# One layer of a gated DeltaNet: the planner's periods become five chains, weights' low halves move to VectorE, an exponential is cut in four, and one more PSUM bank is counted

## The chip, the cores and the metric

The kernel runs on one core of a Trainium2 chip. The metric is the device time of one execution in microseconds; the runs of before took 1149.68, 1152.65 and 1159.56 us, so their median is 1152.65.

## The reference, cut to what matters

With a depth of one only the gated DeltaNet layer runs, on one sequence of 1024 tokens of width 1024, and a final RMS norm follows.

```python
h = rms_norm(x) * (1 + scale(c)) + shift(c)
qkv, z, b, a = split(h @ w_in)                       # q, k: 8 heads; v, z: 16 heads; all of 128
q, k, v = split(silu(causal_depthwise_conv(qkv)))    # 4 taps
q, k = l2norm(q) * 128 ** -0.5, l2norm(k)            # each for two heads of v
beta, g = sigmoid(b), -exp(a_log) * softplus(a + dt_bias)
# by chunk: decay = exp(gc_i - gc_j) below the diagonal, gc the running sum of g
T = inverse(I + strictly_lower((k * beta) @ k.T * decay))
u, w = T @ (v * beta), T @ (k * beta * exp(gc))
# scan over the chunks, state S of 128 x 128 for each head
v_new = u - w @ S
o = (q * exp(gc)) @ S + lower(q @ k.T * decay) @ v_new
S = S * exp(g_last) + (k * exp(g_last - gc)).T @ v_new
o = rms_norm(o) * norm_w * silu(z)
out = rms_norm(x + gate(c) * (o @ w_out))
```

## The kernel before, in words

Chunks are 128 tokens here instead of 64, which changes no result, so the scan of a head has 8 steps. Heads of v go in pairs that share one head of q and k; a pair is a group, and there are 8 groups, G = 0 to 7. Matrices in float32 that need precision are split in a high and a low half in a faster format, and each projection is three products (high by high, high by low, low by high).

Ahead of the groups stand the norm, the modulation and the first projections. Then, for each group:

- `project` (from L591) makes one block of 128 columns for half of the tokens: 24 products of 128x512 into a bank pj (L598). A group has 6 such columns: k and q (`proj_kq`), two of v (`values`), two of z (`out_gate`). `loader` brings the weights: a DMA, ScalarE's high half whi (L586), GpSimd's low half wlo (L587), two of each for a column.
- `Conv` (L537 to L561): ScalarE copies the bank and scales it by one tap, VectorE adds three taps (L557), ScalarE does the SiLU (L561). Values are then transposed on TensorE (L813).
- `norms`: VectorE adds the gates to the mask em (L641), ScalarE takes the exponential of em, 128x2048 at once (L644), and k and q are transposed (L659, L667) for their squares.
- `stage_a`: products of k with k and q (L704), the matrix to be inverted, and the inverse of its 32x32 blocks by 62 short VectorE instructions on tm, tb and ua, each waiting for the one before (L733, L736). This is what the prediction calls the inversion chain. `levels` puts the blocks together on TensorE (L766 to L797), for each half of the tokens.
- `scan`: in each step k @ S into ks (L940), r on VectorE (L943), T @ r into ts (L963), vd (L967) and vh, q @ S into the bank oq (L973), the new state (L982, L987). The second product of a step, into the other half of oq (L910), comes in the next step, and VectorE sums both in o (L913). Then o is normalised over ScalarE, VectorE and GpSimd (L918 to L923), transposed on TensorE into pot (L892) and multiplied with z.

What sets the order: nothing is left to the hardware or the compiler. A planner (`Order`, from L62) runs while the program is built. It keeps a clock `now` for TensorE and a queue for each other engine, with a cost and a rank for each instruction, and emits the instruction of an engine whose planned start comes first, the lowest rank among equals. The work is written as generators, each of which yields a condition (`done`: planned as finished; `free`: a bank counted as free); `drive` steps the first generator whose condition holds. Each engine executes its instructions in the order that came out, whatever the real times are.

Before the change `drive` is called once for each period: the scan of group G, `stage_a` and `values` of G+1 and `proj_kq` of G+2 are given together, and the next period's generators start when all of them are over; only columns of z run on. When the projections are over, the products with the first four blocks of w_out (`early`, L1067) fill TensorE beside the last scan. The rest of w_out follows, 576 products.

Of the kernel before, what the change touches and what calls it, by code (L numbers as in the profile page):

```python
# [17 lines left out]
P = 128  # L18
# [12 lines left out]
RG = 1  # L31
LEV1 = (0, 7)
# [7 lines left out]
LATS, LAT, LATP, DMA = 50, 200, 320, 2800  # L40
# [21 lines left out]
class Order:  # L62
# [67 lines left out]
def gdn_layer(ctx: ExitStack, tc: tile.TileContext, x, c, ada_w, ada_b, norm_g, w_in, conv_w, a_log, dt_bias,  # L130
# [438 lines left out]
    def loader():  # L569
        while True:  # L570
# [9 lines left out]
            for k4 in range(0, KT, 4):  # L580
# [6 lines left out]
                ops.append(pool(lambda raw=raw, ks=ks, hi=hi, lo=lo: nc.gpsimd.tensor_tensor(  # L587
                    lo[:, ks], raw, hi[:, ks].bitcast(F32), op=ALU.subtract), 1290, a, holds=r))
# [22 lines left out]
    class Group:  # L611
        def __init__(self, gi):
# [4 lines left out]
            self.nop, self.TTop = [], {}  # L617

    def proj_kq(gi, G, old):
        G.kq = []  # L620
        for j, ct in ((0, 8 + gi), (1, gi)):
# [8 lines left out]
    def norms(gi, G):  # L630
# [3 lines left out]
        yield lambda: hasattr(order, "gate") and done(*order.gate, order.gc)  # L634
# [9 lines left out]
        G.emop = act(lambda: nc.scalar.activation(em, em, AF.Exp), 1820, *e, table="exp")  # L644
# [42 lines left out]
    def stage_a(gi, G, old):  # L687

        kq, ats = G.kq, []
        if not hasattr(G, "normed"):  # L690
            yield from norms(gi, G)
# [3 lines left out]
        for hf in range(NHALF):  # L695
            em, brk = G.em[hf], G.brk[hf]

            at, ops = None, []
            for j in range(4):
                js = slice(j * P, (j + 1) * P)  # L700
                yield lambda: done(G.emop, G.nop[hf][3]) and free("tr") and (not old or not old.ats or old.inverted[hf])
# [43 lines left out]
    def levels(gi, G, hf, old):  # L745
# [6 lines left out]
        yield lambda: not order.lock and (not (hf and old) or done(old.passed[0]))  # L752
        order.lock = True
# [45 lines left out]
        order.lock = False  # L799
# [4 lines left out]
    order.lock = False  # L804

    def values(gi, G, more):
# [13 lines left out]
        def tiles():  # L820
            for h in range(2):
                ct = 16 + 2 * gi + h
                cv = Conv(ct)
                for hf in range(NHALF):
                    if h == 0:
                        G.vtok.append(cp.tile([P, 4, 2, P], F32, name="vtok", tag="vtok", bufs=3))
                    ps, ph = yield from project(ct * P, hf, hf == NHALF - 1)
                    vT = cp.tile([P, TH], F32, name="vT", tag="vT", bufs=VB)
# [29 lines left out]
    def out_gate(head, G):  # L858

        for hf in range(NHALF):  # L860
            ps, ph = yield from project(Z0 + head * P, hf, hf == NHALF - 1)
            sz = cp.tile([P, TH], F32, name="sz", tag="sz")

            def store(hf=hf, sz=sz):
# [4 lines left out]
                            holds=ph))  # L869
            yield None  # L870

    def scan(gi, G):

        h0 = 2 * gi
        st = cp.tile([P, 2, P], F32, name="st", tag="st", bufs=1)
        late = []

        zs = {}

        def fetch():  # L880

            for n, *_ in late:
                if n not in zs and len(zs) < ZB and G.gated[n // 4] == 2:
                    z = cp.tile([P, 2, P], F32, name="z", tag="z", bufs=ZB)
                    zs[n] = z, load(lambda n=n, z=z: nc.sync.dma_start(
                        out=z, in_=z_dram[h0:h0 + 2, :, n * P:(n + 1) * P].rearrange("h e t -> e h t")))

        def finish():
            n, o, op = late.pop(0)
            pot, held = bank("pot", (P, 2, P)), order.hold("pot", 1)  # L890
            for h in range(2):
                nc.tensor.transpose(pot[:, h], o[:, h], ident)  # L892
            order.now += M2
            oT, stored = cp.tile([P, 2, P], F32, name="oT", tag="oT", bufs=OB), order.hold("oT", 1)
            z, zo = zs.pop(n)
            a = act(lambda: nc.scalar.mul(oT, pot, normw_c), 470, holds=held)  # L896
            b = pool(lambda: nc.gpsimd.tensor_tensor(oT, oT, z, op=ALU.mult), 800, a, zo)  # L897
            load(lambda: nc.sync.dma_start(
                out=o_dram[h0:h0 + 2, :, n * P:(n + 1) * P].rearrange("h e t -> e h t"), in_=oT), b, holds=stored)
            fetch()  # L900

        def can_finish():
            fetch()
            return late and late[0][0] in zs and done(late[0][2]) and free("pot") and order.avail("oT", OB)

        def second(n, po, vh, vo, o, oo):
# [5 lines left out]
            if n > 0:  # L912
                d = vec(lambda: nc.vector.tensor_tensor(o, o, po[:, 1], op=ALU.add), 256, *oo)  # L913
            else:
                d = vec(lambda: nc.vector.tensor_copy(o, po[:, 1]), 256)
# [8 lines left out]
            late.append((n, o, d))  # L924
            fetch()

        pend = sto = None
        for n in range(NT):
# [3 lines left out]
            while len(late) > LAG:  # L932
                yield can_finish
                finish()
# [4 lines left out]
            if n > 0:  # L939
# [7 lines left out]
                if len(late) > 2 and can_finish():  # L947
                    finish()
# [43 lines left out]
        while late:  # L992
            yield can_finish
            finish()
# [236 lines left out]
    with tc.manual_schedule(engines=ORDERED(nc)):  # L1231
# [9 lines left out]
        for gi in range(-1, HQ):  # L1241
# [8 lines left out]
            if gi + 1 < HQ:  # L1250
                if gi < 0:
                    streams.append(streams0)
# [91 lines left out]
```

## Time and profile before

| what | value |
|---|---|
| runs | 1149.68, 1152.65, 1159.56 us |
| profiled execution | 1154.56 us, its span 1152.8 us |
| granted TensorE clock, mean | 0.97 |
| TensorE, VectorE, ScalarE, GpSimd busy | 1075.8, 757.8, 542.7, 440.1 us |
| as shares of the span | 93%, 66%, 47%, 38% |
| chain that ended last, by engine | TensorE 43%, VectorE 23%, ScalarE 11%, DMA 8%, GpSimd 6% |

Engines work side by side, so the shares do not add up. A matmul's end is modelled, and so a wait of TensorE is partly covered in the table by the matmul before it; from start to start it shows whole. Idle time of another engine counts only where TensorE waits for it.

### The profile page before, as it was taken

To read this page: it belongs to the slowest core of one execution; us is meant where nothing else is said; L and a number is where in the kernel's file an instruction comes from. 1 tells how busy PE (TensorE), PEld (TensorE's weight loads), DVE (VectorE), ACT (ScalarE), POOL (GpSimd) and SP (SyncE) were. 2 spreads that over 40 slices of the span, in tenths; PEclk is the share of its full clock that TensorE was granted. 3 is DMA by queue.
4 is the path that set the end of the run, shared out by engine and by line. 5 is a ranking of instruction groups with operands and counts; after the bars stand their busy time and mean duration, and the time that the engine had idled before them with its cause. 6 is when DMAs were issued, how large, how long until landed. Compare 5 with 4: busy or idle time off the path is not lost.

```text
span 1152.8 us, 18300 instructions
## 1 busy us (share of the span) xinstructions
PE 1075.8 (93%) x6295; PEld 859.8 (75%) x6295; DVE 757.8 (66%) x1913; ACT 542.7 (47%) x1415; POOL 440.1 (38%) x530
## 2 busy tenths in 40 slices
PE   7999998989999999899989998999999889999997
PEld 7877786867787777677867786778787657788785
DVE  5458963697789757776686678577767766413514
ACT  6457921443662346336623743374356424424523
POOL 3351321352352115313622452154215234844643
PEclk9899997999999889999999999999999979999999
DMA  9812142233154322421423052215212474335441
GB/s 286 224 37 91 42 119 69 69 102 95 40 150 120 84 78 67 122 69 47 119 61 110 27 148 56 75 39 144 65 56 70 115 231 134 101 114 182 153 128 73
DMA packets 187555, 118.43 MB, mean 103 GB/s; under 512 B 59669, under 2 KB 166470, under 8 KB 186438
## 3 DMA queue, kind: packets, MB, share of 16 engines
q1 hardware_dynamic: 186960, 117.15, 35.7%
q8 instruction: 50, 0.82, 0.3%
q14 instruction: 43, 0.35, 0.1%
q10 hardware_dynamic: 502, 0.10, 0.0%
HBM read 91.98 MB, written 25.24 MB: 102 GB/s over the span
## 4 chain that ended last, share of the span: by engine, by line
PE 43%; DVE 23%; ACT 11%; DMA 8%; issue 6%; POOL 6%; SPq 2%; DVEq 0%; ACTq 0%; POOLq 0%
PE pj L598 20%; DVE tm L733 5%; DVE tb L736 5%; PE pj L1067 4%; DVE vT L557 3%; DMA ua<-D 2%; DVE em L641 2%; DMA woraw<-in_gdn_w_out 2%; POOL wolo L206 2%; PE tr L704 2%; PE tr L797 2%; PE tr L789 2%; ACT tr L662 1%; ACT tr L669 1%; DVE kq L557 1%
## 5 line engine op out<-in xcount | busy, mean ns | idle before, releaser
L587 POOL TENSOR_TENSOR wlo<-wraw,whi 128x512 fp32r<-128x512 f32 x88 | 120.1, 1380 | 301.0 <-ACT whi L586 291.3
L733 DVE TENSOR_TENSOR tm<-tb,ua 128x126 f32<-128x126 f32 (+22 forms) x248 | 81.2, 327 | 25.3 <-DMA ua<-D 18.9
L557 DVE SCALAR_TENSOR_TENSOR kq<-xb,taps,kq 128x512 f32<-128x512 f32 x96 | 76.4, 804 | 22.3 <-ACT kq L554 19.2
L736 DVE TENSOR_TENSOR tb<-tb,tm 128x126 f32<-128x126 f32 (+22 forms) x248 | 82.2, 331 | 6.9
L557 DVE SCALAR_TENSOR_TENSOR vT<-xb,taps,vT 128x512 f32<-128x512 f32 x96 | 82.1, 855 | 5.0 <-ACT vT L554 3.9
L598 PE MATMUL pj<-h0hia,whi 128*128 128x512 f32 x184 | 77.6, 422 | 1.3 <-ACT kq L554 1.3
L598 PE MATMUL pj<-h0loa,whi 128*128 128x512 f32 x184 | 78.6, 427 | 0.0
L598 PE MATMUL pj<-h1lob,whi 128*128 128x512 f32 x184 | 77.4, 421 | 0.0
L598 PE MATMUL pj<-h0hia,wlo 128*128 128x512 f32 x184 | 77.2, 419 | 0.0
L598 PE MATMUL pj<-h0lob,whi 128*128 128x512 f32 x184 | 76.7, 417 | 0.0
L598 PE MATMUL pj<-h1loa,whi 128*128 128x512 f32 x184 | 76.3, 414 | 0.0
L598 PE MATMUL pj<-h1hia,wlo 128*128 128x512 f32 x184 | 76.2, 414 | 0.0
L598 PE MATMUL pj<-h0hib,wlo 128*128 128x512 f32 x184 | 76.0, 413 | 0.0
L598 PE MATMUL pj<-h1hia,whi 128*128 128x512 f32 x184 | 75.3, 409 | 0.0
L598 PE MATMUL pj<-h1hib,whi 128*128 128x512 f32 x184 | 75.3, 409 | 0.0
L598 PE MATMUL pj<-h0hib,whi 128*128 128x512 f32 x184 | 74.7, 406 | 0.0
L598 PE MATMUL pj<-h1hib,wlo 128*128 128x512 f32 x184 | 74.6, 405 | 0.0
L922 POOL TENSOR_TENSOR sso<-sso,neg_half 128x2 f32<-128x2 f32 x64 | 45.6, 713 | 71.4 <-DVE sso L920 67.9
L552 ACT COPY xb<-pj 128x512 f32<-128x512 f32 x62 | 36.1, 582 | 67.4 <-PE pj L598 63.7
L897 POOL TENSOR_TENSOR oT<-oT,z 128x256 f32<-128x256 f32 x64 | 48.1, 751 | 51.7 <-ACT oT L896 44.9
L896 ACT ACTIVATE oT<-pot,cols 128x256 f32<-128x256 f32 x64 | 30.3, 474 | 78.5 <-PE pot L892 76.8
L206 POOL TENSOR_TENSOR wolo<-woraw,wohi 128x512 fp32r<-128x512 f32 x36 | 48.7, 1371 | 44.7 <-ACT wohi L205 44.7
(459 smaller groups left out, 2923.6 us busy)
## 6 DMA issues: line engine op xcount, KB each, us to landing
wraw<-in_gdn_w_in SPq DMA_DIRECT2D x92, 256.0 KB, 3.3
woraw<-in_gdn_w_out SPq DMA_DIRECT2D x50, 256.0 KB, 3.2
wa<-in_ada_w SPq DMA_DIRECT2D x16, 512.0 KB, 7.0
em<-gc_dram SPq DMA_DIRECT2D x8, 1024.0 KB, 5.3
z_dram<-sz SPq DMA_DIRECT2D x32, 256.0 KB, 2.1
z<-z_dram SPq DMA_DIRECT2D x64, 128.0 KB, 2.4
o_dram<-oT SPq DMA_DIRECT2D x64, 128.0 KB, 1.9
gsrc<-o_dram SPq DMA_DIRECT2D x32, 256.0 KB, 3.0
```

The source lines that it names most:

```text
L206: nc.gpsimd.tensor_tensor(lo, raw, hi.bitcast(F32), op=ALU.subtract)
L552: a = act(lambda: nc.scalar.copy(xb[:, NTAP - 1:], ps), 512, *old, rank=0, holds=held)
L557: d = [vec(lambda j=j: nc.vector.scalar_tensor_tensor(dst, xb[:, j:j + TH], tp[:, j], dst, op0=ALU.mult, op1=ALU.add), 512, *d)]
L587: ops.append(pool(lambda raw=raw, ks=ks, hi=hi, lo=lo: nc.gpsimd.tensor_tensor(lo[:, ks], raw, hi[:, ks].bitcast(F32), op=ALU.subtract), 1 ...
L598: nc.tensor.matmul(ps, lhsT=a[:, k], rhs=b[half][k // 4][:, k % 4], start=(k == 0 and n == 0), stop=(k == KT - 1 and n == 2))
L641: e = [vec(lambda n=n, h=h: nc.vector.scalar_tensor_tensor(em[:, h, n], em[:, h, n], ngc[:, n, h0 + h:h0 + h + 1], mask, op0=ALU.add, op1= ...
L733: d = [vec(lambda j=j, mm=mm, ln=ln, tmv=tmv: nc.vector.tensor_tensor(tmv, tb[:, :mm, j:j + 1].to_broadcast([P, mm, ln]), ua[:, j:j + 1, j ...
L736: d = [vec(lambda j=j, mm=mm, tmv=tmv: nc.vector.tensor_tensor(tb[:, :mm, j + 1:], tb[:, :mm, j + 1:], tmv, op=ALU.subtract), 220 + mm * l ...
L896: a = act(lambda: nc.scalar.mul(oT, pot, normw_c), 470, holds=held)
L897: b = pool(lambda: nc.gpsimd.tensor_tensor(oT, oT, z, op=ALU.mult), 800, a, zo)
L922: d = pool(lambda: nc.gpsimd.tensor_tensor(sso, sso, neg_half[:, :2], op=ALU.pow), 700, d)
L1067: nc.tensor.matmul(acc, lhsT=a[:, ts], rhs=b, start=(first and n == 0), stop=(last and n == 2))
```

## The change

The eight periods go. The scans of all groups are one generator after the other, and so are `norms`, `stage_a` (with both halves of `levels`), the filling projections (`proj_kq`, `values`, columns of z in the order of before) and, new as a chain of its own, `outputs`, which transposes and gates the finished rows. All are driven at once until the last is over; what kept a period's work apart is now asked for buffer by buffer (`passed`, `gone`, `free`). The low halves of weights in `loader` are made by VectorE at rank 2. The exponential of em is four instructions of 128x512. The bank oq has a counted hold, so a step is planned only when the sum of the step before has read it. In the planner, an instruction's earliest start is 380 ns instead of 200 after TensorE's clock, and 300 in place of 320 pass between a planned end and `done`.

```diff
-LEV1 = (0, 7)
...
-LATS, LAT, LATP, DMA = 50, 200, 320, 2800
+LATS, LAT, LATP, LATE = 50, 200, 300, 380
+DMA = 2800
...
-        op = Op(eng, cost, fn, [a for a in after if a is not None], rank, table, self.now + LAT)
+        op = Op(eng, cost, fn, [a for a in after if a is not None], rank, table, self.now + LATE)
...
-                ops.append(pool(lambda raw=raw, ks=ks, hi=hi, lo=lo: nc.gpsimd.tensor_tensor(
-                    lo[:, ks], raw, hi[:, ks].bitcast(F32), op=ALU.subtract), 1290, a, holds=r))
+                ops.append(vec(lambda raw=raw, ks=ks, hi=hi, lo=lo: nc.vector.tensor_tensor(
+                    lo[:, ks], raw, hi[:, ks].bitcast(F32), op=ALU.subtract), 720, a, rank=2, holds=r))
...
+        def gone(self):
+
+            return self.left is not None and all(o.end is not None for o in self.left)
...
                 if j == 0:
+                    yield lambda: not old or done(old.passed[hf])
                     G.kq.append(cp.tile([P, 2, TH], F32, name="kq", tag="kq", bufs=4))
...
-        yield lambda: hasattr(order, "gate") and done(*order.gate, order.gc)
+        yield lambda: hasattr(order, "gate") and done(*order.gate, order.gc) and (gi < 2 or Gs[gi - 2].gone())
...
-        G.emop = act(lambda: nc.scalar.activation(em, em, AF.Exp), 1820, *e, table="exp")
+        G.emop = [[act(lambda x=em[:, h, n:n + 4]: nc.scalar.activation(x, x, AF.Exp), 512, *e[2 * n:2 * n + 8], rank=2,
+                       table="exp") for h in range(2)] for n in range(0, NT, 4)]
...
-        yield from levels(gi, G, 0, old)
-        if gi not in LEV1:
-            yield from levels(gi, G, 1, old)
+        yield from levels(gi, G, 0)
+        yield from levels(gi, G, 1)
...
-        yield lambda: not order.lock and (not (hf and old) or done(old.passed[0]))
-        order.lock = True
+        yield lambda: 2 * gi + hf < 3 or done(Gs[gi - 2 + hf].passed[1 - hf])
...
+    def outputs():
+        for _ in range(HQ * NT):
+            yield can_finish
+            finish()
+
     def scan(gi, G):
...
-            while len(late) > LAG:
-                yield can_finish
-                finish()
+            yield lambda: len(late) <= LAG
...
-                if len(late) > 2 and can_finish():
-                    finish()
...
-            yield lambda: hf in G.TTop and done(*ro, G.TTop[hf], G.nop[hf][4], *G.emop2)
+            yield lambda: hf in G.TTop and done(*ro, G.TTop[hf], G.nop[hf][4], *G.emop2) and free("oq")
             TT = G.TT[hf]
-            po = bank("oq", (P, 2, 2, P))
+            po, held = bank("oq", (P, 2, 2, P)), order.hold("oq", 3 if n else 1)
...
-        for gi in range(-1, HQ):
-            running.append(gi)
-            streams, filler = [], []
...
-            must = [Run(g) for g in streams] + [Run(itertools.chain(*filler))]
-            drive(background + must + ([zruns[gi + 2]] if gi + 2 < len(zruns) else []) + [trun] * (gi >= HQ - 2), must)
-        drive(background + [trun], [trun])
+        chain = itertools.chain.from_iterable
...
+        def others(gi):
+
+            if gi + 1 < HQ and gi > 0:
+                yield proj_kq(gi + 1, Gs[gi + 1])
+            yield from itertools.islice(zgates, sum(ZQ[:2]) if gi == 0 else ZQ[gi + 1])
+            if gi == HQ - 1:
+                yield done_projecting()
+
+        zgates = iter(zgates)
+        scans = Run(chain(scan(gi, G) for gi, G in enumerate(Gs)))
+        finishing, last = Run(outputs()), Run(early())
+        drive([Run(loader()), Run(early_loads()), Run(streams0), scans, finishing,
+               Run(chain(stage_a(gi, G) for gi, G in enumerate(Gs))), Run(chain(norms(gi, G) for gi, G in enumerate(Gs))),
+               Run(residual_gate()),
+               Run(chain([proj_kq(1, Gs[1])] + [values(gi, G, chain(others(gi))) for gi, G in enumerate(Gs)])), last],
+              [scans, finishing, last])
```


In the changed kernel the lines carry other numbers (L940 is L948, L733 is L740). Three places of the order that came out follow, each before and then after.

TensorE, the fifth chunk of group 5's scan, from k @ S (ks) to q @ S (oq); pj are projections. Before:

```order
L940 MATMUL ks<-st,kq 128x256
L910 MATMUL oq<-vh,em 128x128 x2
L892 MATMUL pot<-ident,o 128x128 x2
L598 MATMUL pj<-h1hia,wlo 128x512
L598 MATMUL pj<-h1hib,whi 128x512
L963 MATMUL ts<-r,TT_731 128x128 x2
L973 MATMUL oq<-st,kq 128x256
L704 MATMUL tr<-kq 128x256 x2
L982 MATMUL ks<-vd,ktok 128x256
```


After, up to the product that makes the new state:

```order
L948 MATMUL ks<-st,kq 128x256
L921 MATMUL oq<-vh,em 128x128 x2
L893 MATMUL pot<-ident,o 128x128 x2
L711 MATMUL tr<-kq 128x256
L598 MATMUL pj<-h0lob,whi 128x512
L598 MATMUL pj<-h0hib,wlo 128x512
L598 MATMUL pj<-h1hia,whi 128x512
L968 MATMUL ts<-r,TT_731 128x128 x2
L978 MATMUL oq<-st,kq 128x256
L598 MATMUL pj<-h1loa,whi 128x512
L598 MATMUL pj<-h1hia,wlo 128x512
L598 MATMUL pj<-h1hia,whi 128x512
```


Between ks and ts there were the second product of the last step, a transpose of an output and two projections; now a product of k with k and three projections stand there.

VectorE, inside group 3's inversion chain (tm, tb). Before, with a transposed value's scaling and a step of the convolution between:

```order
L733 TENSOR_TENSOR tm<-tb,ua 128x108
L736 TENSOR_TENSOR tb<-tb,tm 128x12x9
L733 TENSOR_TENSOR tm<-tb,ua 128x96
L736 TENSOR_TENSOR tb<-tb,tm 128x12x8
L733 TENSOR_TENSOR tm<-tb,ua 128x91
L816 TENSOR_TENSOR vtok<-tr,rinv 128x4x128
L736 TENSOR_TENSOR tb<-tb,tm 128x13x7
L557 SCALAR_TENSOR_TENSOR vT<-xb,taps,vT 128x512
```


After:

```order
L740 TENSOR_TENSOR tm<-tb,ua 128x96
L557 SCALAR_TENSOR_TENSOR kq<-xb,taps,kq 128x512
L743 TENSOR_TENSOR tb<-tb,tm 128x12x8
L587 TENSOR_TENSOR wlo<-wraw,whi 128x512
L740 TENSOR_TENSOR tm<-tb,ua 128x91
L587 TENSOR_TENSOR wlo<-wraw,whi 128x512
L743 TENSOR_TENSOR tb<-tb,tm 128x13x7
L740 TENSOR_TENSOR tm<-tb,ua 128x78
```


Two low halves of weights (wlo) stand between the steps of the chain now.

ScalarE, at group 4's exponential. Before:

```order
L918 ACTIVATE junk,sso<-o 128x128 x2
L969 ACTIVATE vh<-ts,brk 128x128 x2
L644 ACT_TABLE_LOAD
L644 ACTIVATE em<-em 128x2048
L975 ACTIVATE o<-oq,eall 128x128 x2
L896 ACTIVATE oT<-pot,cols 128x256
L969 ACTIVATE vh<-ts,brk 128x128 x2
```


After:

```order
L650 ACT_TABLE_LOAD
L650 ACTIVATE em<-em 128x512 x2
L974 ACTIVATE vh<-ts,brk 128x128 x2
L874 ACT_TABLE_LOAD
L874 ACTIVATE sz<-pj 128x512
L990 COPY st<-ks 128x256
L650 ACT_TABLE_LOAD
L650 ACTIVATE em<-em 128x512 x2
```


Between two pairs of pieces stands a SiLU of z, with a table load for it and another for the second pair.

## Rows read from the trace of the kernel before

**Rows 1.** Table by stretch: length, busy us of each engine (x instructions), clock, DMA share, GB/s.

```profile
133.00:272.00 139.00, 129.40 (x729) 103.52 (x728) 93.69 (x261) 50.35 (x129) 42.28 (x54) 0.94 0.30 78
272.00:491.40 219.40, 203.75 (x1267) 161.56 (x1266) 165.50 (x462) 105.06 (x300) 77.09 (x101) 0.97 0.36 98
491.40:919.00 427.60, 407.11 (x2580) 326.11 (x2579) 308.80 (x808) 212.78 (x604) 151.26 (x200) 1.00 0.29 80
600.30:709.20 108.90, 102.94 (x652) 82.37 (x651) 78.67 (x204) 53.80 (x153) 39.38 (x51) 1.00 0.30 81
919.00:1010.00 91.00, 81.16 (x512) 62.69 (x511) 53.99 (x120) 35.54 (x101) 49.07 (x52) 0.91 0.50 155
```

**Rows 2.** The chain that ended last: start us, us, what.

```profile
709.19 4.67 PE pj L598 x20
```

**Rows 3.** Waits of TensorE, 600.3 to 709.2: total us, times, longest.

```profile
PE tr L813 <- ACT vT L561: 3.4, 2, 2.8
PE oq L973 <- DVE o L913: 1.3, 1, 1.3
```

**Rows 4.** Timeline of TensorE: start us, us, engine, line, operation [idle before <-releaser].

```profile
698.74 0.40 PE L598 MATMUL pj<-h0hia,whi 128*128 128x512 f32 x1
701.97 0.66 PE L813 MATMUL tr<-ident,vT 128*128 128x128 f32 x4 [2.83 <-ACT vT L561]
702.38 0.48 PE L598 MATMUL pj<-h0loa,whi 128*128 128x512 f32 x1
...
658.05 0.61 PE L910 MATMUL oq<-vh,em 128*128 128x128 f32 x4
658.49 0.38 PE L892 MATMUL pot<-ident,o 128*128 128x128 f32 x2
659.17 0.61 PE L963 MATMUL ts<-r,TT 128*128 128x128 f32 x4
661.09 0.67 PE L973 MATMUL oq<-st,kq 128*128 128x256 f32 x2 [1.31 <-DVE o L913]
```

**Rows 5.** Timelines of VectorE, GpSimd and ScalarE around 690 to 702 us.

```profile
690.52 0.30 DVE L736 TENSOR_TENSOR tb<-tb,tm 128x133 f32<-128x133 f32 x1
690.85 1.27 DVE L733 TENSOR_TENSOR tm<-tb,ua 128x126 f32<-128x126 f32 x1
698.83 0.75 DVE L557 SCALAR_TENSOR_TENSOR vT<-xb,taps,vT 128x512 f32<-128x512 f32 x1
...
690.67 2.60 POOL L587 TENSOR_TENSOR wlo<-wraw,whi 128x512 fp32r<-128x512 f32 x2 [4.59 <-ACT whi L586]
...
701.28 0.63 ACT L561 ACTIVATE vT<-vT 128x512 f32<-128x512 f32 x1 [6.77 <-DVE vT L557]
```

**Rows 6.** Groups of VectorE, the period's and the whole run's: busy us, mean ns | idle before.

```profile
L557 DVE SCALAR_TENSOR_TENSOR vT<-xb,taps,vT 128x512 f32<-128x512 f32 x12 | 10.9, 905 | 0.2
L736 DVE TENSOR_TENSOR tb<-tb,tm 128x126 f32<-128x126 f32 (+22 forms) x32 | 10.4, 326 | 1.0
...
L1041 DVE TENSOR_TENSOR h0hib<-woraw,h0hia 128x512 fp32r<-128x512 f32 x2 | 1.4, 692 | 3.0 <-ACT h0hia L1040 3.0
```

**Rows 7.** Table by stretch at the low clock; timeline of TensorE at the first inversion.

```profile
184.00:204.00 20.00, 18.25 (x127) 14.10 (x128) 5.46 (x14) 3.35 (x7) 2.50 (x2) 0.57 0.27 72
396.00:404.00 8.00, 8.00 (x62) 5.92 (x55) 4.65 (x10) 2.54 (x5) 1.88 (x3) 0.58 0.41 98
416.00:428.00 12.00, 12.00 (x74) 10.14 (x75) 4.36 (x14) 5.10 (x22) 1.09 (x2) 0.72 0.18 56
...
185.06 0.22 PE L766 MATMUL tr<-TE,at 32*32 32x32 f32 x2 [3.48 <-DVE TE L758]
```

**Rows 8.** Groups of GpSimd and ScalarE in 600.3 to 709.2: busy us, mean ns | idle before.

```profile
L587 POOL TENSOR_TENSOR wlo<-wraw,whi 128x512 fp32r<-128x512 f32 x12 | 16.8, 1414 | 41.5 <-ACT whi L586 41.5
...
L644 ACT ACT_TABLE_LOAD x1 | 1.3, 1283 | 0.0
```

**Rows 9.** Timeline of GpSimd.

```profile
664.09 0.61 POOL L923 TENSOR_TENSOR o<-o,sso 128x256 f32<-128x256 f32 x1
```

More of the change, by code (lines that the diff above doesn't have):

```diff
@@ L685, in half_norms, with stage_a @@
             have.append(new)
[L687 to L691, printed above, removed]
+    def stage_a(gi, G):
+        yield lambda: G.nop
+        kq, ats, old = G.kq, [], Gs[gi - 1] if gi else None
         D1 = dram.tile([16, P, 32], F32, name="D1", tag="D1", bufs=2)
@@ L802, in levels @@
         yield None
-    order.lock = False
     def values(gi, G, more):
@@ L868, in out_gate, with fetch @@
             load(store, act(lambda ps=ps, sz=sz: nc.scalar.activation(sz, ps, AF.Silu), 512, rank=0, table="silu",
-                            holds=ph))
+                            holds=ph), holds=held)
             yield None
+    late, zs = [], {}
+    def fetch():
+        for G, gi, n, *_ in late:
+            if (gi, n) not in zs and len(zs) < ZB and G.gated[n // 4] == 2:
+                z = cp.tile([P, 2, P], F32, name="z", tag="z", bufs=ZB)
+                zs[gi, n] = z, load(lambda z=z, n=n, h=2 * gi: nc.sync.dma_start(
+                    out=z, in_=z_dram[h:h + 2, :, n * P:(n + 1) * P].rearrange("h e t -> e h t")))
@@ new lines, in finish @@
+    def finish():
+        G, gi, n, o, op = late.pop(0)
+        pot, held = bank("pot", (P, 2, P)), order.hold("pot", 1)
+        for h in range(2):
+            nc.tensor.transpose(pot[:, h], o[:, h], ident)
+        order.now += M2
+        oT, stored = cp.tile([P, 2, P], F32, name="oT", tag="oT", bufs=OB), order.hold("oT", 1)
+        z, zo = zs.pop((gi, n))
+        a = act(lambda: nc.scalar.mul(oT, pot, normw_c), 470, holds=held)
+        b = pool(lambda: nc.gpsimd.tensor_tensor(oT, oT, z, op=ALU.mult), 800, a, zo)
+        load(lambda: nc.sync.dma_start(
+            out=o_dram[2 * gi:2 * gi + 2, :, n * P:(n + 1) * P].rearrange("h e t -> e h t"), in_=oT), b, holds=stored)
@@ L872, in scan, with can_finish @@
+    def can_finish():
+        fetch()
+        return late and late[0][1:3] in zs and done(late[0][4]) and free("pot") and order.avail("oT", OB)
+    def outputs():
+        for _ in range(HQ * NT):
+            yield can_finish
+            finish()
     def scan(gi, G):
         h0 = 2 * gi
+        yield lambda: (0, 0) in G.vop and (0, 1) in G.vop and done(G.vop[0, 0], G.vop[0, 1])
         st = cp.tile([P, 2, P], F32, name="st", tag="st", bufs=1)
[L876 to L906, printed above, removed]
+        def second(n, po, vh, vo, o, oo, held):
             hf, j = divmod(n, 4)
@@ L988, in scan @@
                               rank=-1)
-            pend = (n, po, vh, vo, o, oo)
+            pend = (n, po, vh, vo, o, oo, held)
             yield lambda: done(*vo)
         second(*pend)
-        while late:
-            yield can_finish
-            finish()
+        G.left = [op for q in order.queue.values() for op in q]
+        yield None
     never = Op()
     def residual_gate():
+        yield lambda: Gs[RG - 1].left is not None
         gate_c = const.tile([P, KT], F32, name="gate_c")
@@ L1071, in gdn_layer @@
     xrs = {}
-    running = []
     def gated_add(acc, yt, tg, t, hf):
@@ L1134, in early_loads @@
             else:
-                yield lambda: HQ - 1 in running and order.early0
+                yield lambda: order.early0 and Gs[HQ - 2].gone()
             for kt in range(EARLY):
@@ L1207, in drive @@
                 assert idle < 20000, [r.gen for r in must if not r.over]
-    def follow(run):
-        while not run.over:
-            yield lambda: run.over or not run.wait or run.wait()
-            run.step()
     order.projecting, order.early0 = True, False
```

61 lines of the change are left out of this document (18 added, 43 removed).

## The prediction

> **What bounds the kernel now.** The busy shares of the page (the table above) only say where to look: TensorE 93%, with the ends of its matmuls modelled. The table by stretch comes next [rows 1]. From 491 to 919 us one period repeats, four groups of nearly 109 us (600.3 to 709.2 is one); before it lie a start and two longer periods, behind it a last group, 919 to 1010 us, without projections. A period has 6.0 us without TensorE work by this view, but more hides under the modelled ends, so I count the work instead. Projections issue every 0.2335 us [rows 2]; 288 of them are 67.2 us. The scan has 37 pairs of products at 0.44 us (658.05 to 658.49 in [rows 4]): 16.3. The 48 transposes take 0.41 us for four (701.97 to 702.38 in [rows 4]): 4.9. Eight products of k with k and q, priced like the scan's, make 3.5, and the inversion's small products about 6, an estimate from half a microsecond to one for each of their eight batches. Together 98 us: a period of 108.9 loses 11, a tenth. TensorE is the bound, and what can be won is what it loses.
>
> Where: the waits of TensorE in this period are 3.4 us on ScalarE's SiLU of vT, 1.3 us on VectorE's sum o, and less on the rest [rows 3]. Start to start the timeline shows them larger: 3.23 us before a transpose of the values where 0.23 would do, and 1.92 in chunk 4 of the scan where 0.44 would do, since the next product into the one output bank oq may not start before o has been summed from it [rows 4]. That is 3.0 and 1.5; a second transpose adds 0.7, four waits at ks and ts of 0.3 to 0.8 us add 1.9. So 7.1 of the 11 have names; the rest are waits too short to list.
>
> Why is the SiLU late? ScalarE stood idle for 6.77 us before it, waiting for VectorE's convolution [rows 5]. VectorE was in the inversion chain ahead of it. A step of that chain takes 0.30 us, but two took 1.27, from 690.85, while GpSimd ran two low halves of weights from 690.67 for 2.60 us [rows 5]. The planner wrote the order for steps of constant length, so 2 us of lateness arrive on TensorE. The mean of the convolution's step on vT says the same: 905 ns [rows 6], against 750 in the instance at 698.83 with GpSimd idle [rows 5].
>
> Last, the granted clock: in three stretches its mean is 0.57, 0.58 and 0.72, that is, much of them at 1.2 instead of 2.4 GHz [rows 7]. The first surrounds a wait of 3.5 us for the first inverse block [rows 7]. A stretch T at mean c loses T(1-c): 8.6, 3.4 and 3.4 us.
>
> **The change, part by part.** *Low halves on VectorE.* Twelve a period leave GpSimd, 16.8 us of its time [rows 8]. VectorE did the same subtraction elsewhere in 692 ns [rows 6]: 8.3 us more a period. What GpSimd's instruction cost it goes: seen are 12 x 0.155 = 1.9 on vT and 1.9 for the one pair in the chain, 3.8 in all; were it blocked for all of GpSimd's time, 16.8. I take 8, an estimate between the two. So VectorE stays near its 78.7 us a period [rows 1], between 70 and 83, of 103: not the bound. The other price of the move is the wait for ScalarE's high half. On GpSimd it was 41.5 us a period [rows 8] and cost nothing; at VectorE's queue it would hold what stands behind. The order has the halves between chain steps, behind the place where the cast should have ended; I take 2 us for the whole kernel, and the upper end is the slower rival.
>
> *Five chains.* Projections now run ahead of or behind a scan as buffers allow, and the order shows wider spacing: in the piece shown, ks and ts have 1.1 us of other work between them before, 1.8 now (counted at the prices above). So the four waits of the scan shrink, 1.9 to 0.9. Values' transposes stand 6.0 to 6.6 us of work behind their projection, where it was 5.1 to 6.0; with VectorE on time I take 3.7 to 1.0. The bank counted: 1.5 to 0.2, for a chunk is now planned behind the sum of the one before. Of the unnamed 4 us I take one away, since an instruction is entered 180 ns later in the plan than before. A period gains 2.7 + 1.0 + 1.3 + 1.0 = 6.0; four of them 24. From 272 to 491 two periods lose 15.7 us idle in the view [rows 1] and 6.8 of clock: 12 and half the clock, 15. From 133 to 272 the order puts 3 us more work ahead of the first inversion, so its 3.5 us of wait go to 0.5; with half of the clock's 8.6 and 1 in the scan, 8. Behind 919 the final products wait for the same loads, gated by the same end of the projections: 0. Before 133: 0. Sum 47.
>
> *Against it.* Outputs are transposed sooner: 8 to 10 us of work stood between a chunk's last product and its transpose for most chunks, now 4 to 7. That row's way over VectorE, ScalarE and GpSimd ends 6.0 us behind the product in the instance of 658.05 (end 658.66, GpSimd's o done at 664.70, [rows 4, 9]). Without low halves in GpSimd's queue it gets shorter; at one chunk in four waiting 0.5 us, 8 us. *The exponential in pieces* has 33 table loads in place of 23 in the program, ten more at 1283 ns [rows 8]: 12.8 us on ScalarE, which is half idle [rows 1]. The ends are 0 and 12.8; I charge 2. With the halves' 2: 12 against.
>
> The profiled execution took 1154.6 us, 1.9 above the median of the runs. 1154.6 - 47 + 12 = 1119.6, so against the median **1118 us**.
>
> **The rivals.** *Denser still*, 1088 us: all named waits go and the clock stays up. Periods give 9 each, 36; the two before 15.7 + 6.8 + 2; the start 13; less 9. For it: the planned lengths then hold on every engine. Against it: in no period of the trace did the short waits vanish.
>
> *Traded waits*, 1148 us: the outputs' transposes take what the values' give back. Place: pot. Price: 64 chunks at 0.5 to 0.6 us are 35 against the 47, less 7 of the other costs. It decides where o comes 7 us or more behind its product. For it: the spacing is halved, and GpSimd's instructions of that row run beside VectorE's chain. In [rows 5] VectorE waited for GpSimd; if GpSimd now waits for VectorE, o comes later. The Trainium skill, page "SBUF — State Buffer", section "Who interferes with whom", says that a VectorE instruction with two SBUF inputs and a GpSimd one that reads SBUF exclude each other, and the second to issue waits. By that rule a low half on VectorE still excludes what stays on GpSimd, and the sum would be this rival's 1148. The rows agree as far as VectorE's waiting goes; no row here shows GpSimd waiting.
>
> *Low halves block VectorE*, slower, 1170 us: a half waits for its cast, the cast for its DMA, and r, vd and st of the scan stand behind it. Place: the pairs in the inversion chain and beside the scan. It takes the gain from 0.4 us for each of 88 (35 us), and at 0.6 (53 us) ends at 1170. Against it: the halves have the lowest rank but one, so the planner puts them where nothing else was due.
>
> **Chances.** Forecast (1100 to 1135) 0.60, denser 0.13, between forecast and no change 0.08, traded 0.11, slower 0.08. About one per cent, 11.5 us, is what a measurement of this kernel can tell from no change. So faster 0.81, same 0.11, slower 0.08. The range leaves out the slower rival and half of the denser one: 1092 to 1147. Its ends hold the unknown prices too: 12.8 us of table loads and 20 more of transposes one way, the 26 that the denser case adds the other.
>
> **What would show it.** Right: periods near 103 us; starts before the values' transposes less than 1.3 us apart; no chain step at 1.27 us beside a low half; TensorE no longer waiting for o at oq. Wrong: waits of TensorE on GpSimd's o above 20 us in all; VectorE idle before wlo, with TensorE waiting on r or vd right behind; or shorter periods with a last group, from the last projection to the first of the final 576 products, well above 91 us.

## The result

The changed kernel takes 1104.47 us (median of 4 runs, 1103.42 to 1107.0) against 1153.28 (4 runs) for the kernel before on the same chip: a ratio of 0.957, 95% interval 0.954 to 0.960, or 49 us. The prediction was 1118 in a range of 1092 to 1147, with 0.81 on faster. The sign and the range hold; the gain is 14 us larger than forecast, and the runs below give most of it to one cause, to which the prediction gave the smaller part. The profiled execution's span is 1105.3 us, 47.5 below that of before.

### The profile page after: what moved, and what is told of

It is laid out like the page before. It is cut to its first block, busy times and chain, and to the rows that moved or that the text cites. A ratio compares the mean times of both kernels' runs of the same rounds, so it can differ in the third digit from the quotient of the medians.

```text
span 1105.3 us, 18335 instructions
## 1 busy us (share of the span) xinstructions
PE 1056.7 (96%) x6295; PEld 853.5 (77%) x6295; DVE 738.2 (67%) x2001; ACT 565.5 (51%) x1449; POOL 334.7 (30%) x442
## 4 chain that ended last, share of the span: by engine, by line
PE 67%; DVE 7%; DMA 7%; POOL 6%; issue 6%; ACT 5%; SPq 1%; DVEq 0%; POOLq 0%; ACTq 0%
PE pj L598 39%; PE pj L1072 3%; POOL wolo L206 2%; PE ts L968 2%; DMA ua<-D 2%; DMA woraw<-in_gdn_w_out 2%; PE oq L921 2%; PE ks L987 2%; PE tr L711 2%; PE ks L948 2%; PE tr L794 1%; PE oq L978 1%; PE tr L802 1%; PE tr L816 1%; DMA D<-tb 1%
## 5 line engine op out<-in xcount | busy, mean ns | idle before, releaser
L557 DVE SCALAR_TENSOR_TENSOR kq<-xb,taps,kq 128x512 f32<-128x512 f32 x96 | 71.2, 750 | 23.4 <-ACT kq L554 20.5
L933 POOL TENSOR_TENSOR sso<-sso,neg_half 128x2 f32<-128x2 f32 x64 | 50.8, 793 | 117.8 <-DVE sso L931 98.9
L740 DVE TENSOR_TENSOR tm<-tb,ua 128x126 f32<-128x126 f32 (+22 forms) x248 | 68.4, 276 | 22.3 <-DMA ua<-D 17.9
L683 POOL TENSOR_TENSOR rinv<-ssk,pos_half 128x4 f32<-128x4 f32 x16 | 17.9, 1117 | 201.9 <-DVE ssk L682 171.8
L557 DVE SCALAR_TENSOR_TENSOR vT<-xb,taps,vT 128x512 f32<-128x512 f32 x96 | 74.1, 772 | 6.4 <-ACT vT L554 6.1
L898 POOL TENSOR_TENSOR oT<-oT,z 128x256 f32<-128x256 f32 x64 | 50.6, 790 | 91.3 <-ACT oT L897 85.6
L598 PE MATMUL pj<-h0loa,whi 128*128 128x512 f32 x184 | 75.3, 409 | 0.0
L743 DVE TENSOR_TENSOR tb<-tb,tm 128x126 f32<-128x126 f32 (+22 forms) x248 | 71.5, 288 | 4.9
L587 DVE TENSOR_TENSOR wlo<-wraw,whi 128x512 fp32r<-128x512 f32 x88 | 61.3, 699 | 11.6 <-ACT whi L586 11.1
L974 ACT ACTIVATE vh<-ts,brk 128x128 f32<-128x128 f32 x128 | 43.7, 365 | 40.4 <-DVE vd L972 21.3
```

The lines of the kernel that those rows point to most:

```text
L557: d = [vec(lambda j=j: nc.vector.scalar_tensor_tensor(dst, xb[:, j:j + TH], tp[:, j], dst, op0=ALU.mult, op1=ALU.add), 512, *d)]
L587: ops.append(vec(lambda raw=raw, ks=ks, hi=hi, lo=lo: nc.vector.tensor_tensor(lo[:, ks], raw, hi[:, ks].bitcast(F32), op=ALU.subtract), 72 ...
L598: nc.tensor.matmul(ps, lhsT=a[:, k], rhs=b[half][k // 4][:, k % 4], start=(k == 0 and n == 0), stop=(k == KT - 1 and n == 2))
L740: d = [vec(lambda j=j, mm=mm, ln=ln, tmv=tmv: nc.vector.tensor_tensor(tmv, tb[:, :mm, j:j + 1].to_broadcast([P, mm, ln]), ua[:, j:j + 1, j ...
L743: d = [vec(lambda j=j, mm=mm, tmv=tmv: nc.vector.tensor_tensor(tb[:, :mm, j + 1:], tb[:, :mm, j + 1:], tmv, op=ALU.subtract), 220 + mm * l ...
L933: d = pool(lambda: nc.gpsimd.tensor_tensor(sso, sso, neg_half[:, :2], op=ALU.pow), 700, d)
```

## The profile after

Of the page of the changed kernel: busy times and the shares of the chain that ended last.

```profile
PE 1056.7 (96%) x6295; PEld 853.5 (77%) x6295; DVE 738.2 (67%) x2001; ACT 565.5 (51%) x1449; POOL 334.7 (30%) x442
...
PE 67%; DVE 7%; DMA 7%; POOL 6%; issue 6%; ACT 5%; SPq 1%; DVEq 0%; POOLq 0%; ACTq 0%
```

VectorE took on 61.3 us of low halves and is still 20 us less busy than before. TensorE's share of the last chain went from 43% to 67%, VectorE's from 23% to 7%.

The changed kernel's table by stretch, columns as in [rows 1], at borders between the same projections:

```profile
129.70:251.60 121.90, 117.02 (x709) 93.68 (x708) 83.81 (x257) 57.07 (x157) 24.62 (x38) 1.00 0.34 91
251.60:443.70 192.10, 187.96 (x1224) 151.88 (x1223) 152.40 (x460) 102.06 (x279) 42.41 (x68) 1.00 0.37 100
443.70:865.50 421.80, 414.22 (x2649) 335.72 (x2648) 329.51 (x939) 239.13 (x660) 107.23 (x169) 1.00 0.32 87
865.50:961.75 96.25, 82.21 (x510) 63.88 (x511) 44.56 (x99) 34.22 (x98) 49.80 (x53) 0.88 0.48 145
```

From 130 to 865 us the clock is at its higher level. Idle time and low clock are now in the last stretch, which is not shorter than before but longer.

Since the two orders put the same work in other places, I compare them by loss: the real start of a product less the TensorE work that stands ahead of it in its own order, at the prediction's prices. What is left is the time in which TensorE waited or ran at the lower clock. Landmarks are projections (blocks of 24 products, from the first) and the products with w_out. A loss is that of its stretch; in the first row, whose other products the prediction has no prices for, only the difference counts.

| stretch | start before | start after | loss before | loss after | gain | predicted, before costs |
|---|---|---|---|---|---|---|
| start to block 8 | 0 | 0 | 25.6 | 23.1 | 2.5 | 0 |
| block 8 to 22 | 133.5 | 129.7 | 22.3 | 10.3 | 12.0 | 8 |
| block 22 to 44 | 266.4 | 251.6 | 30.3 | 12.5 | 17.8 | 15 |
| block 44 to first w_out | 481.3 | 443.7 | 48.4 | 24.6 | 23.8 | 24 |
| first w_out to the final 576 | 921.7 | 865.5 | 19.4 | 27.4 | -8.0 | 0 |
| final 576 | 1009.6 | 961.75 | 0.3 | 0.8 | -0.5 | 0 |

The gains sum to 47.6. The middle two groups (blocks 58 to 82) take 205.4 us, 102.7 each, where they took 109.1; the prediction said 103.

Waits of TensorE in the whole changed kernel, the longest first, to be held against [rows 3]:

```profile
PE tr L771 <- DVE TE L763: 5.3, 1, 5.3
PE pj L1072 <- ACT h0hia L1126: 4.6, 3, 1.9
PE ks L987 <- DVE vd L972: 3.5, 7, 0.9
PE ks L948 <- DVE st L992: 2.9, 3, 1.8
...
PE pot L893 <- POOL o L934: 2.0, 2, 1.8
```

The wait for vT's SiLU and that for o at oq are gone from the list. The feared one, for GpSimd's o at pot, is 2.0 us in all. Transposes of values, as in [rows 4], now follow what is ahead without a gap (TensorE's timeline: 0.23 us from start to start in this one):

```profile
557.72 0.39 PE L598 MATMUL pj<-h0hib,wlo 128*128 128x512 f32 x1
557.95 0.60 PE L816 MATMUL tr<-ident,vT 128*128 128x128 f32 x4
```

VectorE's groups in the whole run, to be held against [rows 6]:

```profile
L557 DVE SCALAR_TENSOR_TENSOR vT<-xb,taps,vT 128x512 f32<-128x512 f32 x96 | 74.1, 772 | 6.4 <-ACT vT L554 6.1
L743 DVE TENSOR_TENSOR tb<-tb,tm 128x126 f32<-128x126 f32 (+22 forms) x248 | 71.5, 288 | 4.9
...
L740 DVE TENSOR_TENSOR tm<-tb,ua 128x126 f32<-128x126 f32 (+22 forms) x248 | 68.4, 276 | 22.3 <-DMA ua<-D 17.9
L587 DVE TENSOR_TENSOR wlo<-wraw,whi 128x512 fp32r<-128x512 f32 x88 | 61.3, 699 | 11.6 <-ACT whi L586 11.1
```

A low half takes 699 ns on VectorE (the 692 of [rows 6]), and a chain step 276 and 288 where the whole run of before had 327 and 331. Of the 496 steps 43 took over 0.6 us before, each of them beside an instruction of GpSimd, 24 beside a low half. Now it is 25, each beside GpSimd again; the only one of 1.27 us stands beside a low half of w_out, which GpSimd still makes. VectorE's timeline of the changed kernel shows one of the shorter ones:

```profile
556.20 0.27 DVE L740 TENSOR_TENSOR tm<-tb,ua 128x110 f32<-128x110 f32 x1
556.38 0.69 DVE L587 TENSOR_TENSOR wlo<-wraw,whi 128x512 fp32r<-128x512 f32 x1
...
560.27 0.71 DVE L740 TENSOR_TENSOR tm<-tb,ua 128x120 f32<-128x120 f32 x1
561.02 0.28 DVE L743 TENSOR_TENSOR tb<-tb,tm 128x120 f32<-128x120 f32 x1
```

GpSimd's timeline beside it:

```profile
556.37 1.44 POOL L933 TENSOR_TENSOR sso<-sso,neg_half 128x2 f32<-128x2 f32 x1 [2.65 <-DVE sso L931]
...
560.06 0.78 POOL L898 TENSOR_TENSOR oT<-oT,z 128x256 f32<-128x256 f32 x1 [1.56 <-ACT oT L897]
```

The step at 560.27 stood beside GpSimd's oT and took 0.71 instead of some 0.28. The other way round, sso at 556.37 took 1.44 us beside a low half; its mean was 707 ns in the steady periods before and is 797 now. So GpSimd does wait for VectorE now. The Trainium skill, page "SBUF — State Buffer", section "Who interferes with whom", has a VectorE instruction with two SBUF inputs and a GpSimd instruction that reads SBUF exclude each other, whichever comes second, and these rows agree (1.44 us against 0.70, 0.71 against 0.28); but TensorE waits for GpSimd's o only 2.0 us.

## The experiments

Ratios are to the kernel before, with 95% intervals; differences in microseconds are to its 1153.3.

**1. All of the change but the chains and the pieces.** The kernel before with the planner's two constants, the bank counted, and

```diff
-                ops.append(pool(lambda raw=raw, ks=ks, hi=hi, lo=lo: nc.gpsimd.tensor_tensor(
-                    lo[:, ks], raw, hi[:, ks].bitcast(F32), op=ALU.subtract), 1290, a, holds=r))
+                ops.append(vec(lambda raw=raw, ks=ks, hi=hi, lo=lo: nc.vector.tensor_tensor(
+                    lo[:, ks], raw, hi[:, ks].bitcast(F32), op=ALU.subtract), 720, a, rank=2, holds=r))
```

> Periods kept; the planner's two constants, the counted bank and the low halves on VectorE added. Theory L (the low halves on GpSimd lengthened VectorE's chain, and that made TensorE late): the larger part of the gain of 49 us is here already, 1120 to 1130, and no chain step on VectorE lasts 1.27 us. Theory C (free chains space dependent work wider): under a third is here, 1138 to 1148. Theory P (the planner's later start alone): as L in time, but then the run with the constants alone shows the same.

1177.68 us, 1.020 (1.013 to 1.028): longer, by about 2%, and outside every range above. TensorE's longest waits in that run:

```profile
PE tr L767 <- DVE TE L759: 20.9, 6, 6.9
PE pot L893 <- POOL o L924: 10.6, 7, 5.7
PE tr L705 <- ACT tr L670: 6.8, 1, 6.8
```

TE is the transpose behind the inversion chain, and its wait was 3.5 us in all before. From the first tm to the last tb the chain takes 27.3 us for group 4 in the kernel before and 33.4 here: no step of it takes more than 0.74 us, but six low halves of some 0.72 us now stand between them. The middle two groups take 111.7 us each.

Most of the loss lies behind them. Block 82 starts 17 us earlier than in the kernel before (807.3 against 824.5), the final 576 products 20 us later (1029.3 against 1009.6). In between TensorE runs out of other work beside the last two inversions; the clock is 0.50 from 850 to 870 us, behind the first of these waits. That wait, then the stretches from block 82 to the last projection and from the first product with w_out to the final ones, columns as in [rows 1]:

```profile
851.34 0.31 PE L767 MATMUL tr<-TE,at 32*32 32x32 f32 x2 [6.87 <-DVE TE L759]
...
807.30:920.22 112.92, 98.77 (x615) 82.58 (x613) 76.35 (x219) 53.12 (x156) 26.87 (x41) 0.88 0.27 72
928.51:1029.25 100.74, 86.00 (x498) 65.97 (x497) 62.01 (x134) 29.62 (x86) 45.98 (x48) 0.81 0.40 126
```

**2. The chains without the move.** The changed kernel with the low halves back on GpSimd (the diff of 1 reversed).

> The changed kernel with the low halves back on GpSimd, planned at 1290 ns there. Theory L: VectorE's chain steps are hit again and the values' transposes wait, 1122 to 1135. Theory C: 1104 to 1112.

1144.4 us, 0.992 (0.988 to 0.995), above both ranges; tm's mean is 321 ns again. Beside GpSimd's subtraction, chains, bank, pieces and constants together give 9 us.

**3 and 4. The constants alone (380 and 300), the counted bank alone,** each in the kernel before.

```diff
-            yield lambda: hf in G.TTop and done(*ro, G.TTop[hf], G.nop[hf][4], *G.emop2)
+            yield lambda: hf in G.TTop and done(*ro, G.TTop[hf], G.nop[hf][4], *G.emop2) and free("oq")
...
-            po = bank("oq", (P, 2, 2, P))
+            po, held = bank("oq", (P, 2, 2, P)), order.hold("oq", 3 if n else 1)
```

> The kernel before with the planner's constants alone (earliest start 380 ns after TensorE's clock, 300 ns to done). Theory P: 1125 to 1135. Theories L and C: 1143 to 1153, at most the short waits of a period shrink by 1 us each.

> The kernel before with the output bank counted alone. By the prediction's term 1.3 us a period over some seven groups: 1141 to 1146. If the wait only moves to another product of the step, 1150 to 1156.

1152.66 us, 1.000 (0.997 to 1.004), and 1153.69, 1.001 (0.998 to 1.005): nothing that shows, from either. Waits of TensorE with the bank counted:

```profile
PE tr L813 <- ACT vT L561: 13.4, 11, 2.0
PE ts L963 <- DVE r L943: 7.7, 9, 1.4
PE oq L910 <- ACT o L975: 5.9, 11, 1.2
```

The wait for o at oq L973 was 7.7 us over the whole run before and is gone, but r went from 2.9 to 7.7 and ScalarE's o from 1.5 to 5.9. VectorE still had GpSimd's subtractions beside it (tm's mean is 364 ns), and TensorE met its lateness elsewhere.

**5 and 6. No subtraction at all.** GpSimd sets the low halves to zero at the same planned cost, in the changed kernel and in the kernel before; the low halves' part of the products is left out.

```diff
-                ops.append(pool(lambda raw=raw, ks=ks, hi=hi, lo=lo: nc.gpsimd.tensor_tensor(
-                    lo[:, ks], raw, hi[:, ks].bitcast(F32), op=ALU.subtract), 1290, a, holds=r))
+                ops.append(pool(lambda raw=raw, ks=ks, hi=hi, lo=lo: nc.gpsimd.memset(
+                    lo[:, ks].bitcast(F32), 0.0), 1290, a, holds=r))
```

> Chains, and the low halves' subtraction on GpSimd replaced by a memset to zero, planned as if it were the subtraction (the low halves of these weights are left out, the order is that of the chains with the low halves on GpSimd). GpSimd then reads nothing where it held VectorE, and VectorE has no new work. Theory L (VectorE held by GpSimd's reads was the cost): 1104 to 1115, chain steps over 0.6 us fall from 41 to about 25. If GpSimd's position in the order or the planner's costs were the cost, it stays at 1138 to 1148.

> The same replacement in the kernel before: periods, its own order, VectorE not held by weights' halves. Theory L without regard to periods: 1118 to 1130, since 3.7 us of waits before the values' transposes and some of the scan go in each of seven periods. If the periods limit by themselves: 1140 to 1150.

1105.24 us, 0.957 (0.954 to 0.961), and 1107.91, 0.959 (0.955 to 0.963); run 6 lies below both of its ranges. The two groups in the kernel before:

```profile
L587 POOL TENSOR_TENSOR wlo<-wraw,whi 128x512 fp32r<-128x512 f32 x88 | 120.1, 1380 | 301.0 <-ACT whi L586 291.3 <-PE tr L797 9.6
L733 DVE TENSOR_TENSOR tm<-tb,ua 128x126 f32<-128x126 f32 (+22 forms) x248 | 81.2, 327 | 25.3 <-DMA ua<-D 18.9
```

And in run 6:

```profile
L587 POOL MEMSET wlo<- 128x512 f32 x88 | 43.8, 528 | 280.0 <-PE pj L598 280.0
L733 DVE TENSOR_TENSOR tm<-tb,ua 128x126 f32<-128x126 f32 (+22 forms) x248 | 67.8, 273 | 28.4 <-DMA ua<-D 22.1
```

In the changed kernel 61 us of low halves on VectorE cost nothing that shows against run 5. In the kernel before, with its periods, their going from GpSimd gives 45 of the 49 us. Without the subtraction, chains, bank, pieces and constants add 2.7 us (run 5 against run 6): by loss they gain 9 between blocks 22 and 44, and give back 6 ahead of block 8 and 6 behind the projections. That GpSimd's own results came late is not the cost: TensorE's waits for GpSimd sum to 6.3 us in the kernel before and to 5.9 in run 6. But two things went from there: the long read of SBUF, and GpSimd's wait for ScalarE's cast.

**7 and 8. The exponential in one piece; planner constants of 200 and 320,** each in the changed kernel.

```diff
-        G.emop = [[act(lambda x=em[:, h, n:n + 4]: nc.scalar.activation(x, x, AF.Exp), 512, *e[2 * n:2 * n + 8], rank=2,
-                       table="exp") for h in range(2)] for n in range(0, NT, 4)]
+        G.emop = [[act(lambda: nc.scalar.activation(em, em, AF.Exp), 1820, *e, table="exp")]] * 2
```

```diff
-LATS, LAT, LATP, LATE = 50, 200, 300, 380
+LATS, LAT, LATP, LATE = 50, 200, 320, 200
```

> The changed kernel with the exponential in one piece of 128x2048. By the prediction's term (ten table loads, 2 us, ends 0 and 12.8): 1101 to 1106. If the pieces matter because one long exponential holds ScalarE's queue and the norms wait for all of it: 1108 to 1118.

> The changed kernel with the planner's constants of before (earliest start 200 ns after TensorE's clock, 320 ns to done). By the prediction 1 us a period: 1109 to 1114. If the constants carry the fit of plan and machine once VectorE keeps time: 1118 to 1130.

1106.16 us, 0.959 (0.955 to 0.962), at the upper end of the first range: the ten table loads more and the pieces cost and give nothing that shows. 1101.47, 0.954 (0.951 to 0.957), below both ranges, is the fastest kernel of the study, by 3 us that its interval does not part from the changed kernel's.

**9 and 10. Which of the two, the read or the wait?** In the kernel before, a memset with a subtraction of 4 columns of each block behind it, which still waits for the cast; and a full subtraction of the raw weights from themselves, which does not wait.

```diff
-                ops.append(pool(lambda raw=raw, ks=ks, hi=hi, lo=lo: nc.gpsimd.tensor_tensor(
-                    lo[:, ks], raw, hi[:, ks].bitcast(F32), op=ALU.subtract), 1290, a, holds=r))
+                ops.append(pool(lambda raw=raw, ks=ks, hi=hi, lo=lo: (nc.gpsimd.memset(lo[:, ks].bitcast(F32), 0.0), nc.gpsimd.tensor_tensor(
+                    lo[:, ks, 0:4], raw[:, :, 0:4], hi[:, ks, 0:4].bitcast(F32), op=ALU.subtract)), 1290, a, holds=r))
```

```diff
-                ops.append(pool(lambda raw=raw, ks=ks, hi=hi, lo=lo: nc.gpsimd.tensor_tensor(
-                    lo[:, ks], raw, hi[:, ks].bitcast(F32), op=ALU.subtract), 1290, a, holds=r))
+                ops.append(pool(lambda raw=raw, ks=ks, lo=lo: nc.gpsimd.tensor_tensor(
+                    lo[:, ks], raw, raw, op=ALU.subtract), 1290, a, holds=r))
```

> The kernel before, with GpSimd's subtraction of the low halves left out: in its place a memset of the same 128x512 to zero, and behind it a subtraction of the first 4 columns alone, which still waits for ScalarE's cast (so nearly all of the low halves' part of the result is left out). The run with the memset alone took 1107.9 us, and in it two things went: the long read of SBUF, and the wait of GpSimd's queue for the cast. Theory L (the read of 1.3 us held VectorE's steps): the read is nearly gone, so 1105 to 1115 us, and VectorE's tm near 280 ns. Theory Q (what stood behind the wait in GpSimd's queue came late): the wait is back, so 1135 to 1153 us, with tm near 280 ns all the same.

> The kernel before, with GpSimd's subtraction taking the raw weights from themselves: it reads as much as before for as long, but does not wait for the cast (the low halves become zero, so their part of the result is left out). The other half of the pair. Theory L (the read holds VectorE): 1140 to 1155 us, with VectorE's tm near 327 ns as in the kernel before and the long steps near 1.2 us still there. Theory Q (the wait in GpSimd's queue): 1107 to 1115 us.

1109.78 us, 0.963 (0.959 to 0.966), with the wait and without the read; 1140.3, 0.989 (0.984 to 0.993), the other way round. Groups of the run with the wait:

```profile
L587 POOL MEMSET wlo<- 128x512 f32 x88 | 46.2, 525 | 200.4 <-PE pj L598 200.4
L587 POOL TENSOR_TENSOR wlo<-wraw,whi 128x16 fp32r<-128x16 f32 x88 | 27.6, 314 | 94.9 <-issue 46.3 <-ACT whi L586 39.0 <-POOL wlo L587 6.2
...
L733 DVE TENSOR_TENSOR tm<-tb,ua 128x126 f32<-128x126 f32 (+22 forms) x248 | 67.4, 272 | 28.4 <-DMA ua<-D 18.9
```

Groups of the run with the read:

```profile
L587 POOL TENSOR_TENSOR wlo<-wraw 128x512 fp32r<-128x512 f32 x88 | 93.3, 1079 | 279.6 <-PE pj L598 196.3 <-DMA wraw<-in_gdn_w_in 83.1
...
L733 DVE TENSOR_TENSOR tm<-tb,ua 128x126 f32<-128x126 f32 (+22 forms) x248 | 77.5, 312 | 27.3 <-DMA ua<-D 18.0
```

It is the read: 93.3 us of it bring 32.4 us over the memset, 120.1 us in the kernel before 45.4, 0.35 and 0.38 for each us; the wait for the cast brings some 2, which is within the noise. Chain steps over 0.6 us are 39 in the run with the read and 18 in the run with the wait. Both runs have zeros for nearly all low halves, so the zeros are not it.

**11 and 12. The tail.** The changed kernel with 200 and 320, and the loads of x's rows for the last stage made to wait for the last group's transposed loads; 12 takes one z column behind the last group as well.

```diff
-ZQ = (3, 2, 2, 2, 2, 2, 2, 1, 0)
+ZQ = (3, 2, 2, 2, 2, 2, 2, 0, 1)
...
-                xop[tg, t] = load(lambda t=t, tg=tg, ts=ts: nc.sync.dma_start(out=ts[t], in_=x[rows_of(tg, t), :]), last)
+                xop[tg, t] = load(lambda t=t, tg=tg, ts=ts: nc.sync.dma_start(out=ts[t], in_=x[rows_of(tg, t), :]), last,
+                                  *Gs[HQ - 1].d2, rank=2)
```

> The changed kernel with planner constants of 200 and 320, and with the loads of x's rows for the last stage made to wait in the order until the last group's inversion has issued its transposed loads. If the tail's 7.7 us come from that load of 5.5 us behind the 512 KB rows on SP's queue: 1094 to 1099 us, with the wait of PE for TE near 882 us gone or under 1 us. If the tail is bound by the chain's arithmetic or by ScalarE's work there: 1100 to 1104 us, as with the constants alone (1101.5).

> The same, with the last column of z's work taken behind the last group instead of behind the one before it, so that PE has dense work beside the last inversion. If PE lacks work there, 2 to 5 us less than the kernel without this: 1090 to 1097 us. If the wait was the load's alone: no difference, 0 to 1 us; if the column then stands ahead of the output's last products, 1 to 4 us more.

1111.92 us, 0.963 (0.959 to 0.967), and 1112.03, 0.965 (0.961 to 0.968): both expectations missed, 10 us above the constants alone. TensorE's timeline in 11:

```profile
894.62 0.22 PE L771 MATMUL tr<-TE,at 32*32 32x32 f32 x2 [1.97 <-DVE TE L763]
...
900.24 0.76 PE L1072 MATMUL pj<-wohi,h0loa 128*128 128x512 f32 x1 [4.13 <-DVE tmp L1180]
```

Its table by stretch, columns as in [rows 1]:

```profile
900.00:920.00 20.00, 19.76 (x142) 15.28 (x144) 7.37 (x17) 1.59 (x4) 7.38 (x7) 0.67 0.16 44
```

The wait for TE is 2.0 us instead of 5.3, but the projection bank now waits 4.1 us for tmp, and the clock behind it is 0.67, 6.6 us lost in this stretch. tmp (the product with the gate's rows) goes into a buffer that is free once GpSimd has added the tmp before it to x's rows. The trace names each step: the rows' load is issued at 894.09, GpSimd's addition waits for it until 898.11, tmp for the addition until 899.40. The rows came late because the edit held them back, so the edit moved the wait. In 12 the wait for TE is gone too, and TensorE waits 6.8 us for the first high half of w_out instead (872.72). A later place for these loads does not help the tail; another remedy was not tried.

## Why the prediction was right, and where not

**Low halves on VectorE.** Right in size: I took 8 us a period for what GpSimd's subtraction held VectorE, between 3.8 and 16.8. VectorE is busy 757.8 us before and 701.3 with the memset, 56.5 over 88 halves, or 7.7 for twelve. What I mis-sized is what this is worth to TensorE. I gave VectorE's punctuality the values' 2.7 us a period and left the rest to chains, bank and spacing. In run 6, with periods, uncounted bank and old constants, a middle group takes 104.2 us: 4.9 of the 6.4 that it gained. That the four periods gained 23.8 us where 24 stood is therefore luck in part: one term was too small, the others too large.

**Five chains.** The spacing and the counted bank were not worth their terms. The bank's 1.3 us a period are zero in the kernel before (run 4); with VectorE on time, where run 6 still has 7.3 us of waits for o at oq, it was not tried alone. All that is not the subtraction comes to 1.5 us a period (104.2 to 102.7). What the chains give is room. With periods the low halves on VectorE lost 24 us (run 1), with chains they cost nothing (the changed kernel against run 5). The order at the inversion points to it: between the last product of k with k or q and the first block of the levels stand 60 to 65 us of other TensorE work for groups 3 to 5 and 52 for group 6 after the change, counted at the prediction's prices; in run 1 it is 54 and 44. With the low halves on GpSimd it is 40 to 44 with periods and 37 to 46 with chains (run 2), so the planner fills this room only where it plans the low halves on VectorE. After the change the chain itself takes 42 to 45 us for groups 3 to 5 against 27 to 31, and nobody waits for it there. The room was not varied by itself, so this account of the 24 us is argued from the order, not shown. I had the slower rival's mechanism (low halves ahead of what is due) at 0.08 because of the rank; run 1 shows that it is real without chains: in each of its middle groups TensorE waits 2.5 us for a TE, and 1.2 of them are two low halves that stand ahead of it in VectorE's queue (from 637.70 in one, while its input landed at 637.55). The counted bank and the constants stand in run 1 too; low halves moved by themselves were not tried, so how much of the 24 us needs those two is open.

**The start.** 12.0 and 17.8 us where 8 and 15 stood. I gave the clock half of its 8.6 and 6.8 us [rows 1, 7]; it came back whole, clock 1.00 in both stretches. The halves that I left out, 4.3 and 3.4, sum to 7.7, about the 6.8 by which these terms were short. I put the first wait for the inverse down to the order, which has more work ahead of it; in run 6, with the order of before, the wait of 3.5 us is down to 0.7 and the clock is 1.00 and 0.99, so VectorE on time is enough for it.

**The costs.** 12 us were charged and hardly any came: waits at pot 2.0 us in all, table loads nothing (run 7), VectorE idle before low halves 11.6 us without a wait of TensorE above 0.5 us behind it. What does show of the halves is one wait of 1.8 us for st (645.09), behind two of them in VectorE's queue. The traded wait on GpSimd was worth its place among the rivals: 10.6 us at pot in run 1, 5.7 of them at once near the end.

**Behind the projections.** Predicted 0, lost 8.0. "The final products wait for the same loads" failed: the last group's inversion now comes while those loads are issued. SP's queue in the changed kernel, issue time and length:

```profile
870.78 0.90 SPq L1155 DMA_DIRECT2D h1loa<-in_x  x2
871.72 2.42 SPq L1155 DMA_DIRECT2D h1lob<-in_x  x2
874.24 0.60 SPq L1125 DMA_DIRECT2D woraw<-in_gdn_w_out  x1
874.94 5.48 SPq L745 DMA_DIRECT2D D<-tb  x2
```

And TensorE's timeline:

```profile
888.25 0.28 PE L771 MATMUL tr<-TE,at 32*32 32x32 f32 x2 [5.30 <-DVE TE L763]
```

The chain's result is issued behind four 512 KB loads of x, and its two issues take 5.48 us; the first product of the levels starts 16.4 us behind the chain's last step instead of 7.0. From the last projection to the final products it is 99 us (862.8 to 961.75) where it was 91: the third of the signs that I had named for being wrong. With the constants of run 8 the wait is 1.1 us and the loss of the stretch 23.0 instead of 27.4. Runs 11 and 12 did not get the rest back, so that the order of these loads is the whole cause is not shown.

So 47 less 12 missed the 47.5 us between the profiled spans by 12, through errors of both signs: 9.3 us too little ahead of block 44, 8.5 too much behind the projections, and 12 of costs that did not come. That the gains before costs summed to 47.6 for a predicted 47 is luck, since the first two errors nearly cancel. The denser rival, 1088 us, would have needed periods at 100; they are at 102.7.

## What to carry to other kernels

When a short dependent chain on one engine slows in steps beside another engine's instruction, cost that instruction by replacing it with one that does not read (a memset) before rearranging anything: here it told 45 of 49 us in one run. Moving work onto the engine of the chain lengthens the chain (27 to 33 us in run 1); here it cost nothing only where TensorE had other work for all of that time, so look for that work in the order first. A wait that disappears from the list without the late engine getting faster can come back at the next place that needs it, as the bank's did in run 4. And look at where a loss lies, not only at its size: run 1 was ahead of the kernel before until its last two groups.

## What the runs showed of the hardware

A GpSimd subtraction of 128x512 from two SBUF inputs made the whole kernel about 0.38 us longer for each us that it ran (45.4 for 120.1), with VectorE busy for 66% of the span and GpSimd for 38%; a GpSimd memset of the same block, 43.8 us in all, left VectorE's tm at 273 ns where it was 327. Taken from one input twice the subtraction ran 1079 ns instead of 1380. Small operands wait as well: 128x2 on GpSimd took 1.44 us instead of 0.70 beside a low half of 0.69 us on VectorE.
